# Second latent head group taken half by half, with the first half's output projection as its filler

## The chip, the cores and the metric

The kernel runs on one core of a Trainium2 chip. The metric is the device time of one execution in microseconds (us), less is better. Five engines work side by side, each on its own queue of instructions in order: PE (matrix products and transposes), DVE (vector work), ACT (activations, copies), POOL (vector work) and SP, which here issues every DMA. They wait for each other through semaphores.

## What is computed

One layer of a hybrid encoder, sequence length 1024, model width 1024, float32 in and out:

```python
mod = silu(c) @ w_ada + b_ada                 # shift, scale, gate for both sub-layers
h = modulate(rmsnorm(x), sh_a, sc_a)
proj = h @ w_in                               # latents (q 256, kv 128, rope key 32) and ca_qkv
q = rmsnorm(q_lat) @ w_q_up                   # 8 latent heads, 96 wide (64 + 32 rotary)
k_nope, v = split(rmsnorm(kv_lat) @ w_kv_up)  # QK-norm, rotary on 32 columns
o_mla = attention(q, k, v)                    # key chunk <= query chunk, chunks of 64
o_ca = chunk_attention(cq, ck, cv, rel_bias)  # 8 heads of 64, band of 9 chunks
x = x + g_a * (concat(o_mla, o_ca) @ w_out)
h = modulate(rmsnorm(x), sh_m, sc_m)
u = causal_dwconv(h @ w_up, conv_w, conv_b)   # 2 x 2816 columns, width 3
x = x + g_m * ((silu(gate) * val) @ w_down)
```

## The kernel before

Tokens lie in eight tiles t = 0..7 of 128. Most products are made from a high and a low part of each operand, three matmuls for one (`gemm3`).

**Stages.** First the modulation vectors and the normed input; then one long attention stage; then the output projection of the latent heads (tiles `op0` to `op7`); then the first pages of the feed-forward, its 22 up-projection tiles, and the down-projection (`dn`).

**Attention stage.** The work is a list of 32 units, `specs`. A unit is one head and one half g of the queries (g = 0: tokens 0 to 511, g = 1: 512 to 1023). Units 0 to 15 are the band heads (tiles `tc`, `sc`, `pvc`); units 16 to 31 are the latent heads, called m00 to m03 (first group) and m10 to m13 (second group), followed by g: m12_1 is the second half of head 2 of group 1. Before, both halves of a head follow each other: m10_0, m10_1, m11_0, and so on to m13_1.

A unit runs in steps:
- `prep` transposes q and k (PE, one shared PSUM bank with the tag T) and splits them (ACT, DVE);
- `guard`, four times: scores of 128 queries into the one buffer S, whose row minimum DVE reduces (`mz`); `mrow` turns the minima into a row of q;
- `st` for each block of 128 keys: scores turned round (`tm`), two exponentials or one and a copy (ACT, POOL: `pm`, `hlm`), the low part by DVE;
- `val`: the product with the values (`pvm`), and after the last block a logarithm, an exponential and a multiplication (`rim`), which is stored in `oT_d` in DRAM.

A g = 0 latent unit has 4 key blocks, a g = 1 unit has 8. While unit n does its `st`, unit n+1 does its guards and unit n+2 its `prep`.

**Fillers.** The other matrix work is a list of generators, `fillers`: v and q/k projections (`ipv`, `ipq`), the latent projection (`mp`, `lt`), the up-projections of both groups (`qu`, `ku`), and `oca`, the output projection of the band heads, whose sums with x go to `part_d`. After each block `pace(cost, ratio)` draws from this list: ratio `R_CA` = 1.42 for band units, `R_MLA` = 0.64 for latent ones. `f_ada` is a side generator for the remaining modulation vectors. `load_wo(0, n, ...)`, which loads and splits the latent half of `w_out`, stands behind the last unit in the program.

**Order.** A scheduler places the instructions of each engine, by readiness in a model of its own and by priority (`tc.high_priority`, `tc.issue_after`), so the order of one engine's queue is fixed when the program is built.

**Behind attention.** `load_o(t)` reads a tile of `oT_d` into `ol` and its part of `part_d` into `x1`; ACT makes `oh`, DVE makes the low part, PE makes `op{t}`, DVE adds it, and the tile is stored to `x1_d`, squared, and scaled to unit mean square. Then `mod_T(k, h, ...)` transposes four tiles of it (`ht_ps2_{k}_{h}`, PSUM tag hT with two buffers), ACT applies the modulation (`hv`), and `bpage` splits it into f16 pages (`b11`, `b21`, ...). `scale_ff(j, pt)` squares the two raw weight tiles of feed-forward tile j on ACT (`wj`), sums them on PE into `pt` (`wss_ps0` and `wss_ps1`, also of tag hT), takes powers on POOL, and scales the weights on ACT; `ff_w(j)` splits them into seven pairs (`wa` to `wg`). The first products are `p1_0`, `p2_0`, `p1_1`, `p2_1`.

## Time and profile before

| | |
|---|---|
| median of 3 runs | 1446.51 us (1445.69 to 1449.16) |
| the profiled execution | 1452.25 us, its span 1450.4 us |
| PE busy | 1308.1 us (90%) |
| DVE busy | 1064.8 us (73%) |
| ACT busy | 803.0 us (55%) |
| POOL busy | 723.0 us (50%) |
| HBM read, written | 122.88 MB, 28.84 MB |

Times in the profile count from the start of the span. A busy PE is not PE at its peak: a matmul's time grows when the granted clock falls, and matmuls overlap.

### The profile page before, as it was taken

The page shows a single profiled execution, that of the slowest core. Times are in us where ns is not written, and L with a number is a line of the kernel's source. Part 1 is how long each engine was busy: PE and PEld are TensorE (multiplying, and loading weights), DVE is VectorE, ACT ScalarE, POOL GpSimd, SP SyncE. Part 2 cuts the span into 40 slices and gives each one's busy share as a digit, 9 for nine tenths or more (in the row PEclk, how much of TensorE's full clock was granted, in tenths as well). Part 3 has the DMA queues.
Part 4 walks back from the last instruction along what each step waited for, and adds up shares of the span by engine and source line. Part 5 has one row for each costly group of instructions (what it writes and reads, how often), then busy time and mean ns, then how long its engine had stood idle before and what let it go on. Part 6 is the DMA issues. An engine that isn't in the chain of part 4 may idle for free.

```text
span 1450.4 us, 20343 instructions
## 1 busy us (share of the span) xinstructions
PE 1308.1 (90%) x7016; PEld 896.4 (62%) x7016; DVE 1064.8 (73%) x1719; ACT 803.0 (55%) x1517; POOL 723.0 (50%) x776
## 2 busy tenths in 40 slices
PE   3769989898888889997897989999999997999998
PEld 2759879776665546564573444444444446888887
DVE  8866766666599876667377998988888876667564
ACT  5446665455667666656466656766666533333332
POOL 5643223332445352535142577666666636666664
PEclk9979999999889879998998999999999999999999
DMA  9331223321111024432541643222221005446543
GB/s 310 116 91 41 72 68 94 97 66 52 51 37 38 13 62 134 131 110 67 203 155 33 223 151 108 90 88 87 84 84 66 30 30 189 145 147 216 188 148 106
DMA packets 83459, 153.04 MB, mean 106 GB/s; under 512 B 8598, under 2 KB 44698, under 8 KB 83356
## 3 DMA queue, kind: packets, MB, share of 16 engines
q1 hardware_dynamic: 83356, 151.75, 32.0%
q8 instruction: 55, 0.90, 0.3%
q14 instruction: 48, 0.39, 0.1%
HBM read 122.88 MB, written 28.84 MB: 105 GB/s over the span
## 4 chain that ended last, share of the span: by engine, by line
PE 57%; DVE 17%; DMA 11%; ACT 5%; issue 4%; POOL 4%; SPq 0%; DVEq 0%; POOLq 0%; ACTq 0%
PE p L1118 7%; PE p L1117 7%; PE p L1119 7%; DMA aw<-w_ada 7%; PE dn L1359 6%; PE dn L1361 5%; PE dn L1360 5%; PE tm L850 3%; DVE aacc L516 2%; DVE adaw L385 2%; DMA wor<-w_out 1%; DVE mz L806 1%; PE tc L850 1%; PE pvm L876 1%; DVE hlc L861 1%
## 5 line engine op out<-in xcount | busy, mean ns | idle before, releaser
L81 POOL TENSOR_TENSOR wds<-wd,wds 128x512 fp32r<-128x512 f32 x88 | 152.4, 1751 | 103.6 <-ACT wds L75 103.6
L1359 PE MATMUL dn<-wds,g 128*128 128x512 f32 x352 | 136.4, 394 | 9.1 <-ACT g L75 9.1
L75 ACT ACTIVATE wds<-wd 128x512 fp32r<-128x512 f32 x88 | 54.7, 624 | 151.7 <-PE dn L1361 150.3
L1360 PE MATMUL dn<-wds,g 128*128 128x512 f32 x352 | 136.3, 389 | 0.0
L1361 PE MATMUL dn<-wds,g 128*128 128x512 f32 x352 | 135.4, 389 | 0.0
L1346 DVE TENSOR_TENSOR wd<-wd,gmbc 128x1024 f32<-128x1024 f32 x44 | 74.3, 1692 | 79.3 <-DMA wd<-w_down 79.3
L516 DVE SCALAR_TENSOR_TENSOR aacc<-aw,cs,aacc 128x256 f32<-128x256 f32 x84 | 45.2, 538 | 58.3 <-DMA aw<-w_ada 58.0
L850 PE MATMUL tm<-qt,kt 96*128 96x512 f16 (+7 forms) x288 | 78.3, 357 | 8.5 <-ACT pm L854 4.6
L861 DVE TENSOR_TENSOR hlm<-pm,hlm 128x512 f16<-128x512 f32 (+1 forms) x96 | 57.9, 612 | 35.7 <-ACT hlm L858 19.0
L1359 PEld LDWEIGHTS dn<-wds,g 128*128 128x128 f32 x352 | 67.0, 191 | 23.5 <-ACT g L75 9.6
L1198 ACT ACTIVATE u<-c,pk,wcv 128x1024 f32<-128x1024 f32 x44 | 52.2, 1232 | 51.1 <-DVE c L1238 43.9
L81 DVE TENSOR_TENSOR g<-gr,g 128x512 fp32r<-128x512 f32 x44 | 73.3, 1667 | 8.2 <-ACT g L75 8.0
L1361 PEld LDWEIGHTS dn<-wds,g 128*128 128x128 f32 x352 | 66.1, 188 | 14.0 <-DVE g L81 0.3
L1360 PEld LDWEIGHTS dn<-wds,g 128*128 128x128 f32 x352 | 66.1, 188 | 13.9
L1199 DVE SCALAR_TENSOR_TENSOR u<-c,wcv,u 128x1023 f32<-128x1023 f32 x44 | 56.0, 1308 | 24.4 <-ACT u L1198 24.4
L850 PEld LDWEIGHTS <-kt 128*128 128x128 f16 (+2 forms) x480 | 47.2, 103 | 40.0 <-issue 22.7
L854 ACT ACTIVATE pm<-tm,scm 128x512 f32<-128x512 f32 (+1 forms) x96 | 54.9, 577 | 28.4 <-PE tm L850 23.2
L854 ACT ACTIVATE pc<-tc,sca 128x512 f32<-128x512 f32 (+3 forms) x96 | 49.9, 522 | 36.5 <-DVE hlc L861 19.2
L861 DVE TENSOR_TENSOR hlc<-pc,hlc 128x256 f16<-128x256 f32 (+3 forms) x96 | 53.5, 562 | 13.1 <-ACT hlc L858 9.0
L77 POOL TENSOR_SCALAR hlm<-pm 128x384 f16<-128x384 f32 (+2 forms) x48 | 24.3, 507 | 75.6 <-ACT pm L854 61.6
L1110 POOL TENSOR_TENSOR wa<-wu,wa 128x512 f16<-128x512 f32 x22 | 35.2, 1599 | 52.2 <-ACT wa L75 52.1
L850 PE MATMUL tc<-qt,kt 128*128 128x512 f16 (+3 forms) x192 | 56.6, 317 | 4.2 <-ACT pc L854 2.1
(461 smaller groups left out, 4545.5 us busy)
## 6 DMA issues: line engine op xcount, KB each, us to landing
wu<-w_up SPq DMA_DIRECT2D x44, 512.0 KB, 4.2
wd<-w_down SPq DMA_DIRECT2D x44, 512.0 KB, 3.6
aw<-w_ada SPq DMA_DIRECT2D x96, 128.0 KB, 2.1
g_d<-u SPq DMA_DIRECT2D x22, 512.0 KB, 2.6
gr<-g_d SPq DMA_DIRECT2D x44, 256.0 KB, 3.0
adaw<-w_ada_a SPq DMA_DIRECT2D x16, 512.0 KB, 4.3
x<-x SPq DMA_DIRECT2D x8, 512.0 KB, 7.3
wq_r<-w_qk SPq DMA_DIRECT2D x32, 128.0 KB, 2.4
```

The costliest lines, as they stand in the source:

```text
L81: return (pool if eng == "p" else dve).tensor_tensor(o, i, f32(hi), op=SUB)
L516: dve.scalar_tensor_tensor(acc[:], w[:], cs[:, k:k + 1], acc[:], op0=MUL, op1=ADD)
L850: last = pe.matmul(s[:, c0:c1], l, m, start=(y == 0), stop=(y == len(todo) - 1))
L854: act.activation(p[:, :w], s[:, :w], AF.Exp, scale=ninv)
L861: dve.tensor_tensor(hl[:, 1, :w], p[:, :w], hl[:, 0, :w], op=SUB)
L1117: pe.matmul(pt, sh, pg[:, 0], start=(k == 0), stop=False)
L1118: pe.matmul(pt, sh, pg[:, 1], start=False, stop=False)
L1119: pe.matmul(pt, sl, pg[:, 0], start=False, stop=(k == 3))
L1346: dve.tensor_tensor(raw[:], raw[:], gmbc[:], op=MUL)
L1359: pe.matmul(pts[t][n], sh, w[n][:, 0], start=(j == 0), stop=False)
L1360: pe.matmul(pts[t][n], sh, w[n][:, 1], start=False, stop=False)
L1361: pe.matmul(pts[t][n], sl, w[n][:, 0], start=False, stop=(j == NF - 1))
```

## The change

- Units 24 to 31 are reordered: m10_0, m11_0, m12_0, m13_0, then m10_1, m11_1, m12_1, m13_1. The four first-half key pages of this group lie in the band heads' value tiles `vca[2]` to `vca[5]`, which are out of use by then.
- Two new fillers at the end of the list: `wo` (the loading and splitting of the latent half of `w_out`) and `out0`, the output projection of token tiles 0 to 3 with its residual addition, mean square and scaling. `out0` may begin when the last g = 0 unit is through its values (`g0_done`). It stores the sum to `x1_d` and the scaled tile to a new DRAM tensor `xn_d`.
- Behind attention only tiles 4 to 7 are projected; the scaled tiles 0 to 3 are read back from `xn_d`. `mod_T` for the first four tiles stands ahead of the loop, both calls of `scale_ff` inside it.
- `pace` takes its ratio from a plan of four stretches of units: 0 to 13, 14 to 21, 22 to 27, 28 to 31.
- The filler `v1` goes behind `qk3` and waits until unit 3 is through its values.

In the order in which the built programs' instructions stand, the PE queue has the output-projection matmuls (24 a tile) so: before, all 192 behind the last unit; after, 24 from the first score product of m10_1 on, 30 from that of m11_1, 24 from that of m12_1, 18 from that of m13_1, and 96 behind the last unit. The `oca` matmuls, 192 in all, begin in m01_0 instead of m02_0, with 170 of them ahead of the first score product of m10_0 instead of 96; the last stand in m10_0 instead of m11_1. Between the first score products of m11_0 and m10_1 the PE queue holds no filler. `wss_ps0` and `wss_ps1` stand one behind the other behind `op7` and `ht_ps2_7_0`, ahead of `p1_0`; before, `wss_ps0` stood among the matmuls of `op2`.

```diff
--- before.py
+++ after.py
@@ -41,7 +41,6 @@
 TB = 1
 HI_ON, HL_BUFS = "pa", 3
 VSCALE = 2.0 ** 14
-R_CA, R_MLA = 1.42, 0.64
 UP_W = 4.0
 
 
@@ -86,6 +85,9 @@
     part_d = dram.tile([NT, P, D], F32, name="part_d")
     ga_d = dram.tile([P, D], F32, name="ga_d")
     x1_d = dram.tile([NT, P, D], F32, name="x1_d")
+    xn_d = dram.tile([NT // 2, P, D], F32, name="xn_d")
+    ss2 = cst.tile([P, NT], F32, name="ss2")
+    r2 = cst.tile([P, NT], F32, name="r2")
     g_d = dram.tile([NF, P, S], F32, name="g_d")
 
 
@@ -713,6 +715,34 @@
                 sp.dma_start(part_d[t][:, n * 512:(n + 1) * 512], o[:])
 
 
+    wo = []
+
+    def f_wo():
+        for n in range(2):
+            wo.append(load_wo(0, n, "a", "v" if n else "p"))
+            yield 0
+
+    def f_out0():
+        for t in range(4):
+            lo = rtile(f"ol{t}", (P, 4, P), F32R)
+            hi = rtile(f"oh{t}", (P, 4, P), F32R)
+            sp.dma_start(f32(lo[:]), oT_d[0:4, :, t * P:(t + 1) * P].rearrange("k p t -> p k t"))
+            x1 = pgtile([P, D], F32, f"x1_{t}")
+            sp.dma_start(x1[:], part_d[t])
+            hi_of("a", hi[:], f32(lo[:]))
+            lo_of("p", lo[:], f32(lo[:]), hi[:])
+            for n in range(2):
+                c = slice(n * 512, (n + 1) * 512)
+                pt = ps.tile([P, 512], F32, name=f"op{t}_{n}", tag="mm", bufs=2)
+                yield from gemm3_f(pt[:], [(hi[:, k], lo[:, k], wo[n][k][:, 0], wo[n][k][:, 1]) for k in range(4)])
+                dve.tensor_tensor(x1[:, c], x1[:, c], pt[:], op=ADD)
+            sp.dma_start(x1_d[t], x1[:])
+            junk = qtile(f"xj{t}")
+            act.activation(junk[:].bitcast(BF16), x1[:], AF.Square, accum_out=ss2[:, t:t + 1])
+            rsqrt_mean(r2[:, t:t + 1], ss2[:, t:t + 1], D)
+            act.activation(x1[:], x1[:], AF.Copy, scale=r2[:, t:t + 1])
+            sp.dma_start(xn_d[t], x1[:])
+
     NK, NQ = 4, 3
     kts = [at.tile([P, 2, 512], F16, name=f"kt{i}") for i in range(NK)]
     qts = [at.tile([P, 2, 512], F16, name=f"qt{i}") for i in range(NQ)]
@@ -757,10 +787,10 @@
         biases[hd] = bg, bt
 
     class Unit:
-        def __init__(u, n, nm, g, band, odd, vst, dst_d, vs):
+        def __init__(u, n, nm, g, band, odd, vst, dst_d, vs, kt=None):
             u.n, u.nm, u.g, u.band, u.odd, u.vst, u.dst_d, u.vs = n, nm, g, band, odd, vst, dst_d, vs
             u.q = qts[n % NQ]
-            u.k = kts[n % NK]
+            u.k = kt or kts[n % NK]
             kpages[nm, g] = u.k
             u.row, u.slot = (64, 1) if band else (QK, 0)
             order = [0, 1, 2, 3] if g == 0 else ([3, 4, 2, 5, 1, 6, 0, 7] if band else list(range(8)))
@@ -915,7 +945,9 @@
     def mla_unit(n, gr, hh, g):
         u = Unit(n, f"m{gr}{hh}", g, False, hh % 2,
                  lambda b: (mv[gr, b // 2], 2 * (b % 2) + hh // 2),
-                 oT_d[2 * gr + hh // 2][64 * (hh % 2):64 * (hh % 2) + 64], ("m", gr))
+                 oT_d[2 * gr + hh // 2][64 * (hh % 2):64 * (hh % 2) + 64], ("m", gr),
+                 vca[2 + hh][:].rearrange("p a b c d -> p (a b c d)")[:, 0:1024].rearrange("p (a b) -> p a b", a=2)
+                 if gr and not g else None)
 
         def prep():
             with tc.high_priority(offset=OFF_S):
@@ -924,7 +956,7 @@
                 act.activation(u.q[:QK, 0], pt[:QK], AF.Copy, scale=sq)
                 dve.scalar_tensor_tensor(u.q[:QK, 1], pt[:QK], sq, u.q[:QK, 0], op0=MUL, op1=SUB)
                 pt = turned(lambda j: mk[gr, (4 * g + j) // 2][:, j % 2, hh, :], QK, f"mk{gr}{hh}_{g}")
-                if gr == 0 and hh < 2:
+                if gr == 0 and hh < 2 or gr == 1 and g == 0:
                     pool.memset(u.k[QK:QK + 1, 0], 1.0)
                 act.activation(u.k[:QK, 0], pt[:QK], AF.Copy, scale=gk_m[:QK])
                 dve.scalar_tensor_tensor(u.k[:QK, 1], pt[:QK], gk_m[:QK], u.k[:QK, 0], op0=MUL, op1=SUB)
@@ -935,18 +967,21 @@
         u.needv = []
         return u
 
-    fillers = [("v0", f_v(0)), ("qk1", f_qk(1)), ("qk2", f_qk(2)), ("v1", f_v(1)), ("qk3", f_qk(3)),
-               ("m", f_m()), ("up0", f_up(0)), ("up1", f_up(1)), ("oca", f_oca())]
+    fillers = [("v0", f_v(0)), ("qk1", f_qk(1)), ("qk2", f_qk(2)), ("qk3", f_qk(3)), ("v1", f_v(1)),
+               ("m", f_m()), ("up0", f_up(0)), ("up1", f_up(1)), ("oca", f_oca()), ("wo", f_wo()), ("out0", f_out0())]
     done = set()
+    spent = {}
     side = [f_ada()]
     nside = [0]
     ca_done = []
     ga_done = []
+    g0_done = []
+    p0_done = []
 
     def fill_step():
         while fillers:
             key, gen = fillers[0]
-            if key == "oca" and not ca_done:
+            if key == "oca" and not ca_done or key == "out0" and not g0_done or key == "v1" and not p0_done:
                 return None
             try:
                 c = next(gen)
@@ -954,7 +989,8 @@
                 done.add(key)
                 fillers.pop(0)
                 continue
-            if key not in ("v0", "up0", "up1", "oca"):
+            spent[key] = spent.get(key, 0.0) + c
+            if key in ("qk1", "qk2", "v1", "qk3", "m"):
                 nside[0] += c
                 while nside[0] > 2000:
                     nside[0] -= 2000
@@ -970,9 +1006,17 @@
                     break
 
     debt = [0.0]
-
-    def pace(cost, ratio):
-        debt[0] += cost * ratio
+    W_IN, W_M, W_UP, W_O = 20.9e3, 35.0e3, 13.0e3 * UP_W, 41.5e3
+    C_CA, C_M0, C_M1 = 8.1e3, 6.6e3, 11.1e3
+
+    plan = [(14, 14 * C_CA, ("v0", "qk1", "qk2", "v1", "qk3", "m", "up0"), 5 * W_IN + W_M + W_UP),
+            (22, 2 * C_CA + 3 * (C_M0 + C_M1), ("up1", "oca"), W_UP + W_O / 3),
+            (28, C_M0 + C_M1 + 4 * C_M0, ("oca",), W_O * 2 / 3),
+            (32, 4 * C_M1, ("wo", "out0"), W_O / 2)]
+
+    def pace(cost, n):
+        i = next(i for i, x in enumerate(plan) if n < x[0])
+        debt[0] += cost * plan[i][3] / plan[i][1]
         while debt[0] > 0:
             c = fill_step()
             if c is None:
@@ -981,7 +1025,8 @@
             debt[0] -= c
 
     specs = [(ca_unit, p, o, g) for p in range(4) for o in range(2) for g in range(2)]
-    specs += [(mla_unit, gr, hh, g) for gr in range(2) for hh in range(4) for g in range(2)]
+    specs += [(mla_unit, 0, hh, g) for hh in range(4) for g in range(2)]
+    specs += [(mla_unit, 1, hh, g) for g in range(2) for hh in range(4)]
     units = [f(n, *x) for n, (f, *x) in enumerate(specs)]
     U = len(units)
     late = []
@@ -994,7 +1039,12 @@
         u, x = late.pop(0)
         if x == 0:
             need(u.needv)
-        return u.val(x)
+        c = u.val(x)
+        if x == len(u.blocks) - 1:
+            for n, flag in ((3, p0_done), (27, g0_done)):
+                if u is units[n]:
+                    flag.append(1)
+        return c
 
     for _ in range(16):
         fill_step()
@@ -1011,7 +1061,6 @@
             v = units[n + 1]
             tasks += [lambda j=j, v=v: v.guard(j) for j in range(4)] + [v.mrow]
         nb = len(u.blocks)
-        ratio = R_CA if u.band else R_MLA
         for x in range(nb):
             cost = u.st(x)
             late.append((u, x))
@@ -1021,17 +1070,16 @@
                 ca_done.append(1)
             while len(tasks) > 6 * (nb - 1 - x) // nb:
                 cost += tasks.pop(0)()
-            pace(cost, ratio)
+            pace(cost, n)
     while late:
-        pace(value(), R_MLA)
-    need(["oca"])
+        pace(value(), U - 1)
+    need(["oca", "wo", "out0"])
     for _ in side[0]:
         pass
 
 
 
 
-    wo = [load_wo(0, n, "a", "v" if n else "p") for n in range(2)]
     att.__exit__(None, None, None)
     att_pg.__exit__(None, None, None)
     psA.__exit__(None, None, None)
@@ -1071,8 +1119,6 @@
         (pool if le == "p" else dve).tensor_tensor(pg[:, 1], v[:], pg[:, 0], op=SUB)
         B[nm, k] = pg
 
-    ss2 = cst.tile([P, NT], F32, name="ss2")
-    r2 = cst.tile([P, NT], F32, name="r2")
     xn2 = {}
     raws, wsc, last = {}, {}, {}
 
@@ -1141,17 +1187,24 @@
         hi = gb.tile([P, 4, P], F32R, name=f"oh{t}", tag="oh", bufs=4)
         sp.dma_start(f32(lo[:]), oT_d[0:4, :, t * P:(t + 1) * P].rearrange("k p t -> p k t"))
         x1 = tb.tile([P, D], F32, name=f"x1_{t}", tag="x1", bufs=8)
-        sp.dma_start(x1[:], part_d[t])
         o_hl[t] = hi, lo
         xn2[t] = x1
 
+    for t in (4, 5):
+        load_o(t)
     for t in range(4):
+        xn2[t] = tb.tile([P, D], F32, name=f"xn{t}", tag="x1", bufs=8)
+        sp.dma_start(xn2[t][:], xn_d[t])
+    sp.dma_start(xn2[4][:], part_d[4])
+    for t in (6, 7):
         load_o(t)
-        if t % 2:
-            load_ff(t // 2)
-    for t in range(NT):
-        if t + 4 < NT:
-            load_o(t + 4)
+        load_ff(t - 6)
+        sp.dma_start(xn2[t - 1][:], part_d[t - 1])
+    sp.dma_start(xn2[7][:], part_d[7])
+    for k in range(ND):
+        mod_T(k, 0, ps2, "hT", 2)
+        bpage("b11" if k < 4 else "b21", k % 4, hf[k, 0], "v")
+    for t in range(4, NT):
         hi, lo = o_hl.pop(t)
         x1 = xn2[t]
         hi_of("a", hi[:], f32(lo[:]))
@@ -1166,15 +1219,11 @@
         act.activation(xj[:], x1[:], AF.Square, accum_out=ss2[:, t:t + 1])
         rsqrt_mean(r2[:, t:t + 1], ss2[:, t:t + 1], D)
         dve.tensor_scalar(x1[:], x1[:], r2[:, t:t + 1], None, op0=MUL)
-        if t == 1:
+        if t == 4:
             scale_ff(0, ps2.tile([P, 512], F32, name="wss_ps0", tag="hT", bufs=2))
-        if t == 3:
-            for k in range(ND):
-                mod_T(k, 0, ps2, "hT", 2)
-                bpage("b11" if k < 4 else "b21", k % 4, hf[k, 0], "v")
             gens[0] = ff_w(0)
             w0 = [next(gens[0]) for _ in range(2)]
-        if t == 4:
+        if t == 5:
             gens[0] = iter(list(gens[0]))
             scale_ff(1, ps2.tile([P, 512], F32, name="wss_ps1", tag="hT", bufs=2))
             gens[1] = ff_w(1)
```

## The prediction

> **What bounds the kernel now.** I read the page first: its forty slices and the chain that ended last.
>
> ```profile
> PE   3769989898888889997897989999999997999998
> PEclk9979999999889879998998999999999999999999
> PE 57%; DVE 17%; DMA 11%; ACT 5%; issue 4%; POOL 4%; SPq 0%; DVEq 0%; POOLq 0%; ACTq 0%
> ```
>
> PE carries most of the chain, and its slices are full in the feed-forward. The change touches the slices from about the thirteenth on (36 us each), where PE stands at 7 to 9. So I cut that part of the span at the first score product of each latent unit, found by counting the `tm` groups. The columns of the windows are length, then busy time and instructions of PE, PEld, DVE, ACT and POOL, then granted clock, DMA share and GB/s.
>
> ```profile
> core 0: us, PE busy (x) PEld busy (x) DVE busy (x) ACT busy (x) POOL busy (x), PEclk, DMA share, GB/s
> 494.80:522.50 27.70, 24.69 (x127) 14.60 (x126) 23.18 (x55) 18.94 (x40) 8.52 (x16) 0.82 0.07 20
> 522.50:590.50 68.00, 62.70 (x339) 41.33 (x338) 46.01 (x88) 40.01 (x75) 29.69 (x35) 0.95 0.37 117
> 590.50:653.40 62.90, 58.87 (x335) 39.55 (x333) 42.47 (x78) 38.78 (x70) 28.22 (x28) 1.00 0.40 125
> 653.40:667.10 13.70, 10.25 (x56) 5.98 (x55) 9.93 (x30) 7.49 (x15) 9.31 (x10) 0.75 0.35 109
> 667.10:682.20 15.10, 12.59 (x68) 6.96 (x67) 12.72 (x22) 11.88 (x21) 8.20 (x8) 0.89 0.14 45
> 682.20:691.90 9.70, 6.11 (x42) 3.99 (x41) 7.07 (x14) 5.86 (x11) 0.98 (x2) 1.00 0.06 14
> 691.90:705.30 13.40, 11.92 (x52) 5.51 (x51) 4.70 (x9) 6.66 (x12) 2.08 (x4) 0.75 0.33 88
> 705.30:707.30 2.00, 0.02 (x1) 0.00 (x0) 0.67 (x1) 1.89 (x4) 0.00 (x0) 1.00 0.00 0
> 707.30:757.20 49.90, 48.99 (x228) 39.58 (x228) 29.31 (x34) 28.56 (x50) 18.34 (x24) 1.00 0.61 228
> 757.20:777.10 19.90, 15.49 (x80) 8.83 (x80) 9.19 (x12) 16.32 (x28) 11.93 (x12) 0.94 0.05 18
> 777.10:799.20 22.10, 15.87 (x53) 5.84 (x52) 21.32 (x36) 13.61 (x22) 0.00 (x0) 0.82 0.23 71
> ```
>
> The rows are: m01; m02 with m03; m10 with m11; m12_0; m12_1; m13_0; m13_1; a gap of 2.0 us; the eight output tiles with the first-half transposes; the way to the second-half pages; these pages. Three things are to be seen. The last two heads, which have no filler left, take 51.9 us, and here PE has room. The output projection is PE's alone: 48.99 of 49.90 busy at full clock. The pages are DVE's: 21.32 of 22.10.
>
> How much room there is depends on the clock, so I cut the filler-free part finer.
>
> ```profile
> 655.40:658.80 3.40, 2.11 (x17) 1.43 (x15) 2.77 (x7) 3.16 (x6) 2.56 (x4) 1.00 0.30 88
> 658.80:665.70 6.90, 5.13 (x18) 2.37 (x18) 5.98 (x17) 3.69 (x8) 5.67 (x7) 0.51 0.29 80
> 689.60:693.00 3.40, 1.71 (x11) 0.77 (x9) 1.98 (x2) 1.80 (x3) 0.00 (x0) 0.99 0.00 0
> 693.00:699.80 6.80, 5.45 (x14) 1.87 (x13) 1.98 (x3) 3.79 (x6) 1.24 (x2) 0.50 0.64 172
> ```
>
> A stretch in which PE is busy for 62% (2.11 of 3.40) or 50% is followed by some 7 us at half clock. PE's busy time in the last two heads is 10.25 + 12.59 + 6.11 + 11.92 = 40.9 us. Of this 5.13 + 5.45 and some 2.7 (a clock of 0.89 means 22% of 15.1 us at half, five sixths of it busy) ran at half speed, so at full clock it is 40.9 - 6.6 = 34.3 us, 17.1 a head. m13_0 ran at full clock: 6.1. A second-half unit then needs 11.0 us of PE (an estimate from these rows).
>
> **What is moved into attention.** The price of an output matmul comes from the stretch where only these and a few transposes run:
>
> ```profile
> 708.40:735.70 27.30, 27.13 (x117) 21.37 (x115) 4.87 (x4) 1.00 0.94 348
> ```
>
> 27.30 / 117 = 0.233 us. Tiles 0 to 3 are 96 matmuls: 22.4 us of PE that leave the full stage behind attention and enter attention as fillers. The question is which gaps they find.
>
> By the built order they find few. The fillers run beside the four second-half units. In the rows above those two units, unfilled, took 15.10 and 13.40 us for 11.0 of PE: 3 us of room each, and part of this is the half clock, not waiting. The first-half units have the larger share of room, 13.70 and 9.70 us for 6.1 each, and the change puts three of them, m11_0 to m13_0, behind each other with no filler at all, because the `oca` matmuls are drawn earlier and end in m10_0.
>
> I sum from the first score product of m01_0, before at 494.8, where 210.5 us of attention remain. The reordered pace does 18 more matmuls of the up-projection ahead of it: 18 x 0.233 = 4, so 498.8. The band units have the same work at other places; I take 0 for them, with 3 us either way.
> - m01 to m03, m10_0 and all 192 `oca` matmuls: 3 x 17.1 + 6.1 + 192 x 0.233 = 102.1 us of PE. Before, m10 and m11 with 96 of them held 34.3 + 22.4 = 56.7 in 62.90 us, 90%; m02 and m03 with 90, and 3 others, 56.0 in 68.00, 82%. I take 88%, nearer the denser row, as fillers are denser now: 116 us (bounds 82% and 95%, the latter being PE's busy share in the better row with a little added: 124.5 and 107.5).
> - m11_0 to m13_0, no filler: 10 us each, near the row of m13_0 (9.70, full clock): 30. The other end is m12_0's 13.70 at clock 0.75: 41. The splits of `w_out`, which stood beside m12, still lie here, so I add a little to 9.70.
> - m10_1 to m13_1 with 96 matmuls: 4 x 11.0 + 22.4 = 66.4 at 90%: 73.8 (69.9 to 81).
>
> 498.8 + 116 + 30 + 73.8 = 718.6: attention ends 13.3 us later than at 705.3 (0 to 40 with all bounds at one end). ACT, DVE and POOL work of the moved tiles (hi, lo, add, square, scale) hides behind PE: in the better row DVE is busy for 42.47 and ACT for 38.78 of 62.90.
>
> **What is new behind attention.** Before, PE passed from the last value product to `op0` in 2.0 us, because the inputs of tiles 0 to 3 had long been loaded. Now the first tile is number 4, which needs the unit that has just ended.
>
> ```profile
> 705.35 0.59 ACT L883 ACTIVATE rim<-pvm 64x512 f32<-64x512 f32 x1 [1.07 <-PE pvm L878]
> 705.98 0.63 ACT L884 ACTIVATE rim<-rim 64x512 f32<-64x512 f32 x1
> 706.63 2.19 ACT L75 ACTIVATE oh<-ol 128x512 fp32r<-128x512 f32 x4
> 706.63 0.76 DVE L885 SCALAR_TENSOR_TENSOR rim<-pvm,vabm,rim 64x512 f32<-64x512 f32 x1 [1.64 <-ACT rim L884]
> 707.42 0.45 SPq L886 DMA_DIRECT2D oT_d<-rim  x1
> oT_d<-rim SPq DMA_DIRECT2D x5, 128.0 KB, 2.2
> cl<-oT_d SPq DMA_DIRECT2D x15, 256.0 KB, 3.0
> ```
>
> Logarithm, exponential, multiplication: the store is issued 2.1 us behind the last product. It lands 2.2 later; SP issues in order, and `ol4` stands behind it, as do `xn0` to `xn3`, `x1_4` and the first weights. The load of the same kind and size takes 3.0, its high part 0.6. So PE waits 2.1 + 2.2 + 3.0 + 0.6 = 7.9 us, and no transposes stand ahead of `op4` in its queue to fill that. The rows on the clock have some 7 us at half clock behind a lull, which can cost 3.4; some of it lies in the gap itself, so I add 1.5 us. Then 96 x 0.233 = 22.4. In the 49.90 us row 192 output matmuls take 44.7, which leaves 5.2 for 36 others, 0.144 each: the 32 first-half transposes cost 4.6. The end of `ht_ps2_7_0`, before at 757.20 or 51.9 us behind attention, now comes 7.9 + 1.5 + 22.4 + 4.6 = 36.4 us behind it: 15.5 us won.
>
> Part of this is lost at once. `wss_ps0` and `wss_ps1` share the two buffers of tag hT with the transposes, and as `mod_T` is now written ahead of `scale_ff`, both stand behind `ht_ps2_7_0` on PE and ahead of `p1_0`. Before, only `wss_ps1` did, with its squares long done.
>
> ```profile
> 754.66 1.22 DVE L1163 TENSOR_TENSOR x<-x,op 128x1024 f32<-128x1024 f32 x1 [0.18 <-PE op L171]
> 758.82 0.61 PE L1097 MATMUL wss_ps<-wss,ones 128*128 128x1 f32 x4 [1.57 <-ACT hv L1065]
> 759.28 0.38 PE L1117 MATMUL p<-b,wa 128*128 128x512 f16 x1
> 760.54 1.06 POOL L1099 TENSOR_TENSOR wss<-wss,phalf 128x1 f32<-128x1 f32 x1 [1.54 <-DVE wss L1098]
> 761.67 0.55 POOL L1100 TENSOR_TENSOR wss<-wss,nhalf 128x1 f32<-128x1 f32 x1
> 762.26 2.19 ACT L1105 ACTIVATE wu<-wu,wss 128x1024 f32<-128x1024 f32 x2 [1.27 <-POOL wss L1100]
> 764.35 0.61 ACT L75 ACTIVATE wa<-wu 128x512 f16<-128x512 f32 x1
> 764.48 0.69 DVE L1126 TENSOR_TENSOR ws<-wu,wu 128x512 f32<-128x512 f32 x1 [2.68 <-ACT wu L1105]
> 765.20 1.55 DVE L1128 TENSOR_TENSOR wu<-wu 128x512 f32<-128x512 f32 x1
> 766.85 1.46 DVE L1129 TENSOR_TENSOR wu<-wu,wu 128x512 f32<-128x512 f32 x1
> L1095 ACT ACTIVATE wj<-wu 128x1024 bf16<-128x1024 f32 x5 | 5.2, 1045 | 7.2 <-DMA wu<-w_up 7.2
> ```
>
> The new chain, from the end of `op7`: add 1.22, two powers 1.06 + 0.55 with 0.3 about them, so 2.5 us behind the last transpose (0.6 later than `op7`); two scalings 2.19; DVE 0.69 + 1.55 + 1.46; the four splits `wd` to `wg`, 0.61 each, 2.4; and on the same ACT queue only then the two squares for tile 1, 2.5 with their reads. Sum 13.3, and 0.3 for `wss_ps1`: `p1_0` starts 13.6 us behind the last transpose, before 759.28 - 757.20 = 2.1. ACT's copies of the second half (`hv`) stand behind all this, so the DVE-bound pages, before 19.9 us behind, come 31: 11 us lost. From there on the order is the old one, and so is the length.
>
> Last product to pages: before 2.0 + 49.9 + 19.9 = 71.8, now 36.4 + 31 = 67.4, a gain of 4.4 us. If the splits find ACT and DVE free earlier, up to 15.5; if SP's loads come late, a loss of 1.
>
> **Sum.** 13.3 - 4.4 = 8.9 us longer: 1452.25 + 8.9 = 1461.1 for an execution like the profiled one, which lay 5.7 above the median; against the median, 1446.51 + 8.9 = 1455.4.
>
> **The rivals.** A measurement of this kernel tells about 0.3% (4.3 us) from no change; faster is below 1442.2, slower above 1450.8.
> - *The gaps swallow the moved tiles* (faster). Place: m01 to m13_1. If PE reaches 95% wherever it has fillers, the sum is 498.8 + 107.5 + 29.1 + 69.9 = 705.3: attention ends when it did, and the 4.4 behind it are the whole effect, 1442.1; each us of the chain behind `op7` that turns out hidden comes off too, down to 1431. It decides at an end of attention of 705. For it: six heads ran with room in all rows. Against it: 82 and 90% are what this pipeline reached with fillers at hand. Chance 0.22.
> - *Little moves*: attention ends at 705 to 714: chance 0.15.
> - *The filler-free units fall to half clock* (slower than forecast). Three units like m12_0 cost 41 instead of 30: 11 us more, 1466. For it: PE is busy for 6.1 of 9.7 us in such a unit, 63%, and a 62% stretch preceded half clock above. Against it: m13_0 itself stood at 1.00. Chance 0.23. The Trainium skill, page "TensorE: Matmul & The Clock Gate", section "What's actually happening", says that the half clock comes after at least one idle window of about 3.4 us; by that rule no unit that keeps PE partly busy would fall, and these three would cost 29. The trace differs: both stretches ahead of the half clock had PE busy for half of the time and more.
> - That the change doesn't do what it says is ruled out by the built order, which has all 96 matmuls ahead of the last unit's end.
>
> The forecast proper (1451 to 1461) has 0.40. So faster 0.22, same 0.15, slower 0.63. The range leaves one in ten on each side: 1441 to 1469.
>
> **What would show it.** In the profile after: attention's last value product at about 719; three g = 0 units of about 10 us with no filler; a gap on PE of about 8 us behind that product with `oh` as releaser; the last first-half transpose some 36 us behind attention; `p1_0` some 13 us behind it, with `wss` and `wj` ahead. An end of attention below 708, or `p1_0` within 4 us of the transposes, would make the forecast wrong; so would a clock of 0.75 in the filler-free units.

## The result and the profile after

| | before | after |
|---|---|---|
| median of 4 runs each, side by side | 1447.84 us (1445.69 to 1450.23) | 1461.88 us (1461.22 to 1462.69) |
| ratio to before, 95% interval | 1 | 1.0097 [1.0077, 1.0116] |
| the profiled execution | 1452.25 us, span 1450.4 | 1461.27 us, span 1459.5 |
| PE busy | 1308.1 us (90%) | 1302.8 us (89%) |

The change makes the kernel 14 us slower. On another chip the ratio was 1.0104 [1.0083, 1.0125]. The two profiled executions differ by 9.0 us only, because that of before lay 4.4 us above its median and that of after 0.6 below.

The page of after, its slices for PE and the shares of the chain that ended last:

```profile
PE   3769998999877799879767899999999997999998
PEclk9979999999998999989888999999999998999999
PE 63%; DVE 16%; DMA 8%; POOL 4%; ACT 4%; issue 4%; SPq 0%; DVEq 0%; ACTq 0%; POOLq 0%
```

The units without fillers now lie in slices 17 and 18, which read 8 and 7 where before had 9 and 9; before had its own in slice 19, now filled (9 instead of 7). Slices 20 and 21 read 7 and 6 instead of 8 and 9: the output projection has lost its full stage, to the gap behind attention and to the wait ahead of the feed-forward. PE's busy time in all is the same to 0.4%: the work lies elsewhere.

The stages of after, cut at the same landmarks as before (length, then busy time and instructions of PE, PEld, DVE, ACT and POOL, then granted clock, DMA share and GB/s):

```profile
core 0: us, PE busy (x) PEld busy (x) DVE busy (x) ACT busy (x) POOL busy (x), PEclk, DMA share, GB/s
488.50:610.40 121.90, 110.92 (x585) 72.85 (x585) 79.64 (x145) 67.35 (x123) 57.23 (x59) 0.96 0.45 145
610.40:619.70 9.30, 6.45 (x42) 3.97 (x42) 6.24 (x14) 7.00 (x13) 7.92 (x8) 1.00 0.25 83
619.70:632.00 12.30, 7.69 (x44) 4.84 (x44) 11.25 (x17) 7.67 (x14) 7.52 (x7) 0.86 0.29 96
632.00:646.10 14.10, 9.47 (x53) 5.64 (x51) 11.50 (x19) 6.92 (x13) 4.05 (x5) 0.76 0.09 28
646.10:716.40 70.30, 67.16 (x362) 42.79 (x361) 44.07 (x74) 45.23 (x81) 17.35 (x28) 1.00 0.22 76
716.40:725.00 8.60, 0.39 (x2) 0.30 (x2) 2.56 (x14) 2.51 (x4) 0.55 (x1) 0.72 0.46 149
725.00:753.40 28.40, 28.37 (x131) 23.06 (x131) 12.89 (x17) 15.50 (x27) 2.23 (x6) 0.90 0.79 293
753.40:784.70 31.30, 17.47 (x83) 9.46 (x83) 14.02 (x15) 23.31 (x39) 23.14 (x22) 0.78 0.04 18
784.70:806.00 21.30, 13.47 (x50) 4.83 (x49) 20.64 (x34) 12.84 (x22) 0.00 (x0) 0.92 0.21 68
```

The rows are: m01 to m10_0 with all `oca`; m11_0, m12_0 and m13_0 without a filler; the four g = 1 units with 96 output matmuls; the gap; `op4` to `op7` with the first-half transposes; the way to the second-half pages; these pages. Attention ends at 716.4, before at 705.3: 11.1 us later. From there to the pages it takes 68.3 us, before 71.8. The net, some 7.5 us, stays constant through the feed-forward: `p1_6` starts at 906.9 against 899.4, the first down-projection product at 1213.0 against 1205.5. The last 1.6 us of the two spans' difference come in the down-projection, which the kernels share.

How PE's gap behind attention comes about, in the timeline of after (start, length, engine, line, operation; in brackets the idle time before and what ended it):

```profile
715.92 1.15 ACT L743 ACTIVATE x<-x,r 128x1024 f32<-128x1024 f32 x1
717.09 0.59 ACT L913 ACTIVATE rim<-pvm 64x512 f32<-64x512 f32 x1
...
719.15 0.45 SPq L916 DMA_DIRECT2D oT_d<-rim  x1
...
721.38 0.92 SPq L1188 DMA_DIRECT2D ol<-oT_d  x2
...
724.35 0.63 ACT L74 ACTIVATE oh<-ol 128x512 fp32r<-128x512 f32 x1 [6.01 <-DMA ol<-oT_d]
725.03 0.79 PE L171 MATMUL op<-wo,oh 128*128 128x512 f32 x1 [7.64 <-ACT oh L74]
```

It is the forecast chain: logarithm, store at 719.15, load issued once the store has landed (2.2 us later), landing 3.0 later, high part, `op4`. New in it is the scaling of tile 3 (L743), 1.15 us on ACT ahead of the logarithm.

And the chain ahead of `p1_0`:

```profile
755.95 2.19 ACT L1151 ACTIVATE wu<-wu,wss 128x1024 f32<-128x1024 f32 x2
...
762.22 0.63 ACT L74 ACTIVATE wd<-wu 128x512 f16<-128x512 f32 x1 [2.49 <-DVE wu L1175]
...
764.32 1.04 ACT L1141 ACTIVATE wj<-wu 128x1024 bf16<-128x1024 f32 x1
...
765.50 0.59 PE L1143 MATMUL wss_ps<-wss,ones 128*128 128x1 f32 x2 [11.77 <-ACT wj L1141]
```

PE's product waits 11.77 us for the squares, which stand on ACT behind the scaling and the four splits of tile 0.

### The profile page after: what moved, and what is told of

Read it like the earlier page. It is cut to its first block, busy times and chain, and to the rows that moved or that the text cites. A ratio compares the mean times of both kernels' runs of the same rounds, so it can differ in the third digit from the quotient of the medians.

```text
span 1459.5 us, 20393 instructions
## 1 busy us (share of the span) xinstructions
PE 1302.8 (89%) x7016; PEld 893.8 (61%) x7016; DVE 1060.6 (73%) x1715; ACT 806.9 (55%) x1521; POOL 733.5 (50%) x784
## 4 chain that ended last, share of the span: by engine, by line
PE 63%; DVE 16%; DMA 8%; POOL 4%; ACT 4%; issue 4%; SPq 0%; DVEq 0%; ACTq 0%; POOLq 0%
PE p L1163 7%; PE p L1164 7%; PE p L1165 7%; PE dn L1408 5%; PE dn L1409 5%; PE dn L1410 5%; DMA aw<-w_ada 4%; PE tm L880 2%; DVE adaw L387 2%; PE tc L880 1%; DVE aacc L518 1%; PE op L171 1%; PE op L172 1%; PE op L173 1%; DVE mz L836 1%
## 5 line engine op out<-in xcount | busy, mean ns | idle before, releaser
L891 DVE TENSOR_TENSOR hlm<-pm,hlm 128x512 f16<-128x512 f32 (+1 forms) x96 | 68.2, 716 | 36.2 <-ACT hlm L888 18.4
L74 ACT ACTIVATE wd<-wu 128x512 f16<-128x512 f32 x22 | 13.8, 629 | 84.9 <-DVE wu L1175 84.9
L891 DVE TENSOR_TENSOR hlc<-pc,hlc 128x256 f16<-128x256 f32 (+3 forms) x96 | 48.8, 515 | 14.3 <-ACT hlc L888 7.4
L171 PE MATMUL ipq<-wq_s,hT 128*128 128x256 f32 x192 | 57.1, 298 | 0.0
L1249 DVE SCALAR_TENSOR_TENSOR u<-c,wcv,u 128x1022 f32<-128x1022 f32 x44 | 56.3, 1312 | 0.0
```

The costliest lines, as they stand in the source:

```text
L74: return act.activation(o, i, AF.Copy)
L171: pe.matmul(pt, sh, mh, start=(start and i == 0), stop=False)
L891: dve.tensor_tensor(hl[:, 1, :w], p[:, :w], hl[:, 0, :w], op=SUB)
```

## The experiments

All ratios are to before on the same chip, with a 95% interval. The runs were made on four chips; the medians of before were 1452 to 1453 us there, so ratios are compared across chips and traces only by lengths of stages. "Behind attention" means from the last value product to the start of the second-half pages (DVE's `t3_0`, 0.6 us behind the start of the last row above); this is 68.9 us in after and 72.4 in before.

### One suspected wait each: the scale chain

`e1_own_psum`: the sums of `scale_ff` get PSUM buffers of their own, paid for with one buffer of `op`.

```diff
-        pt = ps2.tile([P, 1024], F32, name=f"op{t}", tag="op", bufs=3)
+        pt = ps2.tile([P, 1024], F32, name=f"op{t}", tag="op", bufs=2)
...
-            scale_ff(0, ps2.tile([P, 512], F32, name="wss_ps0", tag="hT", bufs=2))
+            scale_ff(0, ps2.tile([P, 512], F32, name="wss_ps0", tag="w", bufs=2))
... (the same for wss_ps1)
```

> The changed kernel with PSUM buffers of its own for the two sums of squares (wss_ps0, wss_ps1), and two instead of three for the output tiles, so that the scale chain of the first feed-forward tiles no longer stands behind the last transpose. Theory (the chain is on the path): the first product follows the last first-half transpose by 3 us instead of 14.1, the second-half pages come 9 to 11 us earlier, and the kernel takes about 1452 (1450 to 1455) against 1461.9 of the changed kernel. Rival (the pages wait for something else, such as DVE or the copies on ACT): p1_0 moves, the pages do not, and the time stays at 1460 to 1463.

Measured: 1459.85 us, ratio 1.0053 [1.0034, 1.0073], about 6.4 us less than after (1.0097), give or take 4 by the two intervals. From the end of attention in this run to the pages:

```profile
719.10:727.80 8.70, 0.45 (x4) 0.31 (x3) 2.62 (x16) 2.58 (x4) 0.55 (x1) 0.69 0.50 153
727.80:756.30 28.50, 28.50 (x132) 23.14 (x132) 15.15 (x19) 18.51 (x32) 7.34 (x11) 0.91 0.77 290
756.30:781.40 25.10, 16.71 (x80) 9.02 (x80) 12.54 (x13) 19.48 (x34) 18.59 (x18) 0.85 0.06 22
```

The third stage is 25.1 us instead of 31.3, with `p1_0` 7.4 behind the last transpose instead of 14.1; the two others are as in after. The shared PSUM tag is a cause, smaller than the theory had it.

### The wait for the last unit

`e4_no_last_wait`: tiles 4 to 7 read the columns of tokens 0 to 511, stored long before.

```diff
-        sp.dma_start(f32(lo[:]), oT_d[0:4, :, t * P:(t + 1) * P].rearrange("k p t -> p k t"))
+        sp.dma_start(f32(lo[:]), oT_d[0:4, :, (t - 4) * P:(t - 3) * P].rearrange("k p t -> p k t"))
```

> The changed kernel in which the four output tiles behind attention read the columns of tokens 0 to 511 instead of 512 to 1023 of the latent heads' output: that part of the computation is replaced so that no load waits for the last unit's store. Theory (the wait of 8.6 us between the last value product and op4 is on the path): the gap shrinks to 2 to 3 us and the time to about 1456 (1454 to 1458). Rival (the loads of the first-half tiles and weights, or the scale chain behind op7, would be waited for anyway): 1460 to 1463.

Measured: 1460.19 us, 1.0052 [1.0033, 1.0072]. The gap, cut as before:

```profile
720.60:723.70 3.10, 0.39 (x3) 0.30 (x2) 1.46 (x6) 3.02 (x5) 0.55 (x1) 1.00 0.78 256
```

3.1 us instead of 8.6, and the clock at 1.00 instead of 0.72; behind attention 64.1 instead of 68.9. The round trip through DRAM costs 4.8 us by the two traces and some 6.5, give or take 4, by the ratios.

`e7_psum_tile3` tries to fill that gap: on top of `e1_own_psum`, tile 3 is projected behind attention, ahead of tile 4.

```diff
-        for t in range(4):          # f_out0
+        for t in range(3):
...
-    for k in range(ND):
-        mod_T(k, 0, ps2, "hT", 2)
-        bpage("b11" if k < 4 else "b21", k % 4, hf[k, 0], "v")
-    for t in range(4, NT):          # behind attention
+    for t in range(3, NT):
... (and the order of the loads)
+        if t == 3:
+            for k in range(ND):
+                mod_T(k, 0, ps2, "hT", 2)
+                bpage("b11" if k < 4 else "b21", k % 4, hf[k, 0], "v")
```

> The changed kernel with PSUM buffers of its own for the sums of squares, and with token tile 3 left to be projected behind attention: its 24 matmuls need no unit of the second half and can cover the wait for the last one. Theory (the wait is on the path and is covered by 5.6 us of matmuls, while attention loses as many): 4 to 7 us below the run with the PSUM buffers alone, a ratio to before of 1.000 to 1.003. Rival (the wait is covered, but the tile costs behind attention what it saved within): 1.004 to 1.007.

Measured: 1461.41 us, 1.0068 [1.0047, 1.0089], nothing gained over `e1_own_psum`.

```profile
723.20:725.10 1.90, 0.00 (x0) 0.00 (x0) 0.63 (x1) 1.83 (x3) 0.00 (x0) 1.00 0.00 0
725.10:771.00 45.90, 38.41 (x161) 30.43 (x162) 22.70 (x27) 25.55 (x43) 18.68 (x23) 0.85 0.59 221
771.00:790.70 19.70, 16.30 (x76) 7.95 (x74) 8.14 (x10) 14.88 (x26) 9.40 (x8) 0.91 0.01 1
```

The gap is gone (1.9 us), but the first-half transposes, which now need tile 3's mean square, end 47.8 us behind attention instead of 37.0. Of the 68.1 us behind attention (62.9 in `e1_own_psum`) PE idles 7.5 in the second stage.

### The pacing and the order alone

`e2_pace_only`: before, with `v1` behind `qk3` and its gate, and a plan of two stretches, of which the first is the changed kernel's; nothing else is moved.

```diff
-    fillers = [("v0", f_v(0)), ("qk1", f_qk(1)), ("qk2", f_qk(2)), ("v1", f_v(1)), ("qk3", f_qk(3)),
+    fillers = [("v0", f_v(0)), ("qk1", f_qk(1)), ("qk2", f_qk(2)), ("qk3", f_qk(3)), ("v1", f_v(1)),
...
+            if key == "oca" and not ca_done or key == "v1" and not p0_done:
...
+    plan = [(14, 14 * C_CA, 5 * W_IN + W_M + W_UP),
+            (32, 2 * C_CA + 8 * (C_M0 + C_M1), W_UP + W_O)]
```

> The kernel before with one part of the change alone: v1 behind qk3, and fillers paced by a plan (the first stretch as in the change, then up1 and oca spread over all units from 14 on). Order of units, output projection and the end are as before. Theory (the new pacing of the first stretches is a gain of its own, since the changed kernel reached m01_0 6.2 us earlier with 18 more matmuls done): 4 to 10 us faster than before, 1438 to 1444. Rival (the profiled execution of before lost those microseconds by chance; it lay 4 above its median): within 3 us of before, 1445 to 1451.

Measured: 1445.83 us, 0.9952 [0.9933, 0.9970], 7 us faster than before.

`e5_order_only`: `e2_pace_only` with units 24 to 31 half by half as in after, and no output projection in attention.

```diff
-    specs += [(mla_unit, gr, hh, g) for gr in range(2) for hh in range(4) for g in range(2)]
+    specs += [(mla_unit, 0, hh, g) for hh in range(4) for g in range(2)]
+    specs += [(mla_unit, 1, hh, g) for g in range(2) for hh in range(4)]
... (and the key pages in the band heads' value tiles, as in after)
```

> The kernel of the pacing run (v1 behind qk3, up1 and oca spread from unit 14 on, whole output projection behind attention) with one more part of the change: units 24 to 31 half by half. Nothing is projected as a filler. Theory (the order by itself costs nothing; what costs is the moved tiles, the wait for the last unit and the scale chain): the same ratio to the kernel before as the pacing run, 0.995 (0.993 to 0.998). Rival (short units one behind the other are slower than short and long ones by turns): 6 to 12 us more than the pacing run, a ratio of 0.999 to 1.004, with m11_0 to m13_0 taking over 12 us each though they have fillers.

Measured: 1443.84 us, 0.9949 [0.9930, 0.9969]: next to 0.9952 the order costs nothing that these intervals could show. From the first score product of m01_0 to the end of attention, the windows of before, `e2_pace_only`, `e5_order_only`, after, and after on another chip (`a1_changed_again`), one fence each:

```profile
494.80:705.30 210.50, 187.12 (x1007) 117.93 (x1005) 146.08 (x291) 129.62 (x241) 87.00 (x102) 0.92 0.30 94
```
```profile
491.50:698.70 207.20, 184.32 (x1001) 117.21 (x1000) 141.89 (x280) 128.46 (x238) 86.81 (x99) 0.93 0.31 96
```
```profile
490.00:697.00 207.00, 181.70 (x1001) 115.17 (x1000) 148.07 (x282) 128.06 (x238) 88.27 (x100) 0.96 0.31 96
```
```profile
488.50:716.40 227.90, 201.68 (x1082) 130.09 (x1081) 152.69 (x265) 134.17 (x243) 94.06 (x105) 0.96 0.34 111
```
```profile
495.60:724.70 229.10, 202.34 (x1082) 130.42 (x1081) 152.68 (x264) 134.13 (x243) 92.86 (x105) 0.95 0.34 111
```

Between `e5_order_only` and after stand the moved projection and the later stretches of the plan: PE is busy 20.0 us longer and the stage is 20.9 us longer, nearly the 22.4 us of the moved matmuls. PE's idle time is 25.3 and 26.2 us: no gap was filled.

> The changed kernel once more, beside the kernels of this call and the kernel before on the same chip. Both theories: a ratio to before of 1.008 to 1.012, as in the first measurement.

The second look at after: 1468.88 us, 1.0104 [1.0083, 1.0125]. Attention from m01_0 on has the same length within 1.2 us, but m01_0 starts at 495.6 instead of 488.5.

`e9_quarter_mm` removes most of the moved matmuls where they are: of each tile's four products in attention one is computed, 24 matmuls instead of 96.

```diff
-                yield from gemm3_f(pt[:], [... for k in range(4)])
+                yield from gemm3_f(pt[:], [... for k in range(1)])
```

> The changed kernel whose four filler tiles make only one of the four head pairs' products: 24 matmuls instead of 96 in attention; loads, splits, additions, squares, scalings and stores as changed (that part of the projection is left out). Theory (PE has no room beside the second-half units, so each moved matmul costs its 0.233 us there): attention ends 72 x 0.233 = 16.8 us earlier, at least 13, and the ratio to before falls from 1.010 to about 0.998 to 1.001. Rival (it is the other work of these tiles, the waits of the queues or the loads, that lengthens attention): attention ends at most 6 us earlier, a ratio of 1.005 or more.

Measured on the chip of `a1_changed_again`: 1454.20 us, 1.0016 [1.0002, 1.0029], 0.88% less than after there, 12.8 us (give or take 4). Attention ends 11.0 us earlier (713.7 instead of 724.7), less than the 13 that the theory asked for, but nearer to it than to the rival's 6. The four g = 1 units of `a1_changed_again` and of `e9_quarter_mm`:

```profile
654.20:724.70 70.50, 67.15 (x362) 42.81 (x361) 43.96 (x73) 45.16 (x81) 17.30 (x28) 1.00 0.21 75
```
```profile
653.20:713.70 60.50, 55.45 (x292) 30.83 (x291) 43.65 (x86) 46.03 (x81) 18.47 (x29) 0.94 0.28 96
```

72 matmuls less, at 0.233 us 16.8, take 11.7 off PE's busy time and 10.0 off the length. A part of their price stays because PE, with fewer fillers, has more idle time (5.1 instead of 3.4) and a lower clock (0.94 instead of 1.00). So three quarters of the matmuls' price is time of the kernel (12.8 of 16.8). The loads, splits, additions and scaling of the moved tiles are still there; what they cost by themselves was not tried.

### More even fillers

`e3_oca_late`: after, with `oca` drawn later, so that it reaches the units m11_0 to m13_0.

```diff
-            (22, ..., ("up1", "oca"), W_UP + W_O / 3),
-            (28, ..., ("oca",), W_O * 2 / 3),
+            (22, ..., ("up1", "oca"), W_UP - W_O / 6),
+            (28, ..., ("oca",), W_O * 0.8),
```

> The changed kernel with the second and third stretch of the plan lowered, so that the band output matmuls reach into m11_0 (38), m12_0 (28) and m13_0 (6) instead of ending in m10_0; everything else as changed. Theory (the three units without fillers leave 17 us of PE room or half clock that fillers can use): attention ends 5 to 10 us earlier, 1452 to 1457. Rival (these units are bound by their own chain of score, exponential and row minima, and each filler makes them longer): the units grow by what they get, and the time stays within 3 us of 1461.9.

Measured: 1464.44 us, 1.0090 [1.0070, 1.0109], no gain. The units m11_0 to m13_0 run with fillers, 210 matmuls instead of 136, and the g = 1 units start at 644.8, 4.0 earlier than in `e1_own_psum` on the same chip; these give it back:

```profile
597.80:644.80 47.00, 39.36 (x210) 26.39 (x210) 28.52 (x55) 23.55 (x44) 15.37 (x17) 0.95 0.55 182
644.80:720.90 76.10, 71.77 (x364) 44.14 (x363) 48.98 (x87) 48.81 (x85) 28.96 (x37) 0.94 0.26 87
```

The second row was 70.3 us long, PE busy 67.16 at clock 1.00; now 76.1 with 71.77 at 0.94. Why the clock fell there wasn't tried apart.

`e10_pace_even` does the like for the faster kernel below: `W_UP + 0.8 * W_O` in the second stretch of its plan, so that `oca` lasts into m12_1.

> The pacing run with own PSUM buffers, with the plan of its second stretch lowered so that the band output matmuls last into m12_1 instead of ending in m12_0. Theory (the unfilled units at the end leave PE room, which the same matmuls use better there than in the units that are full): 3 to 6 us faster, a ratio to before of 0.988 to 0.991. Rival (what the last units gain the earlier ones lose, as where the changed kernel's band matmuls were drawn later): 0.992 to 0.994.

Measured: 1443.95 us, 0.9946 [0.9928, 0.9964]: no gain either.

### Which part of the pacing gains, and a faster kernel

`e12_plan_only`: `e2_pace_only` with `v1` back ahead of `qk3` and without its gate. At this rate of fillers `v1` overwrites two value tiles (`vca[0]` and `vca[1]`) before the first pair of band heads has used them, so this run computes a part of the band attention from other values. Its instructions are the same, but their waits are not: value products of c01_1, the last unit of that pair, now stand behind these writes.

```diff
-    fillers = [..., ("qk2", f_qk(2)), ("qk3", f_qk(3)), ("v1", f_v(1)),
+    fillers = [..., ("qk2", f_qk(2)), ("v1", f_v(1)), ("qk3", f_qk(3)),
...
-            if key == "oca" and not ca_done or key == "v1" and not p0_done:
+            if key == "oca" and not ca_done:
```

> The pacing run without its first part: v1 stays ahead of qk3 and has no gate, only the pace follows the plan. Theory (the rate makes the gain): the same ratio to before as the pacing run, 0.993 to 0.997, with m00_0 at 456 to 461 as there. Rival (the place of v1 makes it): within 0.2% of before, with m00_0 at 464 to 467 as in the kernel before.

Measured: 1461.35 us, 1.0062 [1.0044, 1.0079], slower than before, which neither theory had. The stretch from c11_0 to c20_0 is 42.8 us in `e2_pace_only`, and here:

```profile
252.30:304.90 52.60, 46.95 (x351) 41.07 (x349) 32.41 (x78) 28.40 (x64) 16.16 (x27) 1.00 0.28 77
```

It holds 351 matmuls instead of 283. c11_0 starts 10.6 us later than in `e2_pace_only` and c20_0 20.4; half of this is won back by m00_0 (470.5 instead of 460.6), and the other 10 stay to the end of attention (708.6 instead of 698.7). A part of this loss is the run's own. The value products of c01_1 stop at 193.43 and go on at 225.63, behind the writes of `v1`:

```profile
193.43 0.27 PE L878 MATMUL pvc<-hlc,vca 128*128 128x256 f16 x1
...
223.52 0.61 DVE L479 SCALAR_TENSOR_TENSOR vca<-ipv,vabc,vca 128x128 f16<-128x128 f32 x2 [0.69 <-ACT vca L477]
...
225.63 0.23 PE L876 MATMUL pvc<-hlc,vca 128*128 128x128 f16 x1
```

Its last multiplication comes at 229.7, in `e2_pace_only` at 201.8. So the run doesn't price the plan alone: the gain of 7 us belongs to the plan together with `v1`'s place and gate, and what each of them gives stays open.

`e0_before_again`: before, once more.

> The kernel before, profiled once more, since its profiled execution (1452.25) lay above the median of its other runs (1446.51 to 1447.84 on that chip). Theory (the attention stage of the kernel before varies by some us from run to run): the units between m00_0 and m02_0 start at other times than in the first profile, relative to c31_1. Rival (they do not): the same stretch of 52 us between the starts of c31_1 and m00_0.

Measured: 1453.37 us, span 1451.5. The 52.4 us from c31_1 to m00_0, the part of before that the new pacing shortens most (43.8 in after), is no accident of one execution:

```profile
413.50:465.60 52.10, 38.87 (x181) 27.40 (x181) 48.13 (x146) 35.58 (x93) 30.50 (x61) 0.87 0.13 34
```

DVE is busy for 48.13 of these 52.10 us.

`e8_pace_psum` puts the two edits together that gained: the pacing of `e2_pace_only` and the PSUM tag of `e1_own_psum`, in before's order.

> The pacing run with PSUM buffers of their own for the two sums of squares and two instead of three for the output tiles. There the first product already follows the last transpose by 1.5 us. Theory (ACT is what the second-half pages wait for, and the scalings and splits of feed-forward tile 1 now run beside the output tiles): the pages come 3 to 6 us earlier, a ratio to before of 0.991 to 0.993. Rival (the pages follow the last output tile whatever ACT has to do): 0.995 as without, or slower if two output buffers hold up PE.

Measured: 1441.40 us, 0.9930 [0.9904, 0.9956]: it beats both kernels, before by 10 us and after by some 24. Whether the PSUM tag adds to the pacing stays open: `e2_pace_only` had 0.9952 [0.9933, 0.9970], and behind attention the two profiles show 71.0 and 70.7 us. That fits the old order, in which only `wss_ps1` stood behind the transposes.

## Why the prediction was right or wrong

The predicted 1455.4 us were 6.5 short of 1461.88, which lies inside the range and just above the forecast proper of 1451 to 1461. Of the 6.5 us 1.3 are the base, as before took 1447.84 beside it and not 1446.51: a loss of 8.9 us was forecast and one of 14.0 measured. The sign and the main mechanism were right (few gaps for the moved tiles, two new waits behind attention), but the terms of the attention stage were not, and that the sum came this near is partly luck. Point by point:

- **Behind attention: right.** The gap is 8.6 us (forecast 7.9, and the clock in it 0.72, for which 1.5 were added to what follows); the last transpose ends 37.0 us behind attention (36.4); `p1_0` starts 14.1 behind that (13.6), the pages 31.3 (31). Together 3.5 us are won, forecast 4.4. `e4_no_last_wait` and `e1_own_psum` show both losses, each by taking a part of it away. The share of the PSUM tag was oversized: the sum put 11 us down to it, and the pages come 6.2 earlier without it (25.1). The 5 us that remain over before's 19.9 were not taken apart.
- **The price of the moved tiles: the step failed in its parts.** From m01_0 to the end of attention the forecast was 116 + 30 + 73.8 = 219.8 us. It took 227.9, 229.1, and 228.4 in both `e1_own_psum` and `e4_no_last_wait`. By terms in after: 121.9 for 116, 35.7 for 30, 70.3 for 73.8. In the first term PE's work was mis-sized: it was busy for 110.9 us, not 102.1. I took 17.1 us of PE for a head and 6.1 for a g = 0 unit from m12 and m13, the last heads of before. These lack the guards and transposes that a unit does for its successors: m12 and m13 held 213 matmuls in one window, so 106.5 a head. The seven units m01 to m10_0 of after hold 393 without the 192 `oca`; three heads of 106.5 and a unit of 42 would be some 362. At 17.1 / 106.5 us each the 31 are 5.0 us; and the clock of 0.96, 8% of the 121.9 us at half, adds up to 4.9. The prediction's own rows had shown it: PE was busy for 62.70 of 68.00 and 58.87 of 62.90 us, 92 and 94%, where 17.1 a head made 56.0 and 56.7, or 82 and 90%. (The 56.0 also counts 90 `oca` matmuls beside m02 and m03; the trace has 96, so 57.4 or 84%.) So the 88% was a share of too small a need, and the 91% that PE was busy in after is no better packing than before's. In the last term the need was right (67.16 us measured, 66.4 forecast), and PE was busy for 95.5% of the time instead of 90.
- **Filler-free units: part of the rival that they fall to half clock.** 11.9 us each instead of 10, at clocks 1.00, 0.86 and 0.76. The two falls of the clock in after, in windows that are cut at them and in PE's timeline:

```profile
624.64:628.05 3.41, 0.43 (x2) 0.10 (x1) 3.37 (x5) 3.18 (x7) 2.43 (x3) 1.00 0.00 0
628.05:631.47 3.42, 2.92 (x9) 1.60 (x10) 3.31 (x6) 1.17 (x2) 1.27 (x1) 0.50 0.57 189
...
634.88:638.29 3.41, 1.71 (x14) 1.26 (x14) 3.00 (x4) 2.81 (x5) 2.19 (x2) 1.00 0.09 33
638.29:641.70 3.41, 1.40 (x5) 0.88 (x6) 3.40 (x7) 1.61 (x5) 0.00 (x0) 0.50 0.00 0
```
```profile
626.36 0.38 PE L820 MATMUL sm<-vca,qt 96*128 96x512 f16 x1 [1.88 <-DVE mz L836]
...
628.29 1.14 PE L766 MATMUL mrm_ps<-ident,mz 128*97 128x128 f32 x4 [1.49 <-DVE sm L835]
...
636.71 0.33 PE L820 MATMUL sm<-kt,qt 96*128 96x384 f16 x1
640.30 0.61 PE L820 MATMUL sm<-vca,qt 96*128 96x512 f16 x1 [3.26 <-DVE mz L836]
```

  PE waits for the row minimum (`mz`) on DVE, which is busy for 3.37 of the 3.41 us ahead of the first fall. Without a filler these units are DVE's more than PE's: 6.24 + 11.25 + 11.50 = 29.0 us of 35.7. The Trainium skill, page "TensorE: Matmul & The Clock Gate", section "HAM oscillation — how this bites in real kernels", puts the limit at no idle gap of over about 3.4 us. Here no wait over 1.88 us lies ahead of the first fall, and at the second PE had waited for 1.25 us (637.04 to 638.29); the rest of the 3.26 came after it. Of the 3.41 us ahead PE was busy for 0.43 and 1.71, 13 and 50%. So the measurement decides, and it speaks for a share of busy time in a stretch, not for one long gap.
- **Band units and pacing, "I take 0": wrong.** With 18 more up matmuls ahead of it, m01_0 started at 488.5 in the profiled run instead of 498.8. `e2_pace_only` shows the pacing without the rest of the change: 0.48% or 7 us, outside my 3 us either way. Half of it comes after m01_0: 207.2 us from there to the end of attention instead of 210.5.
- **Why 13.3 looked right.** The end of attention moved by 11.1 us in the profiled pair, close to the forecast, because a stretch 8 us too long was offset by a start 10 us too early. The start scatters: 488.1 to 496.8 in the seven traces of after and of the runs built on it, 494.8 and 494.4 in the two of before. Over the four runs whose attention is unchanged (716.4, 724.7, 719.1, 720.6) the mean is 720.2, over before's two 704.7: 15.5 later, and 3.5 to 4.3 won behind it, so some 12 us. That is inside the interval of the measured 14 (11 to 17). The first profiled pair shows 9 because before's execution lay above its median; in which stage it did, one trace can't tell. What makes the start scatter was not tried.
- **The rivals.** That the gaps swallow the tiles is excluded: PE's idle time in attention is the same with and without them. That little moves is excluded too.

The balance in shares of the time: pacing -0.5% and the order 0 (`e2_pace_only`, `e5_order_only`), the moved projection with its two waits +1.5% or some 21 us (1.0097 or 1.0104 against 0.9949). The two waits that `e1_own_psum` and `e4_no_last_wait` take away, 6.4 and 6.5 us, are within this, and so is what the shorter output stage gives back.

## What to carry to other kernels

Work moved beside a pipeline that already keeps its engine busy for nine tenths can cost nearly its full time there (here 20.9 us of stage for 22.4 us of matmuls), and frees that time elsewhere only if nothing else stands behind it: compare the engine's idle time with and without the moved work, not its share. A stage that took only inputs stored long ago must not be cut so that its first tile needs the newest result, and two users of one rotating PSUM tag are bound to the order in which the program names them. A change made of several edits is worth splitting: here the pacing with the new place of `v1`, which looked like an accessory, was the only part that by itself made the kernel faster.

## What the runs showed of the hardware that was not expected

The clock of TensorE fell to half with no long wait of PE ahead of it: of the 3.41 us before the two falls PE was busy for 0.43 and 1.71 us, and its longest waits there were 1.88 and 1.25 us. Two executions of after, on two chips, differ by 7.1 us within the first 490 us (m01_0 at 488.5 and 495.6), while the following 228 us of attention repeat within 1.2.
